# Keeping the results of seven batches in SBUF and storing them once, behind all loads

## The chip, the cores and the metric

The kernel runs on one core of one Trainium2 chip. The metric is the time of one execution on the device in microseconds (us), the median of several runs. The profile is of one execution; its span, from the first to the last instruction of the program, is some 1.8 us shorter than that time. The engines are PE (matmul), DVE (VectorE), ACT (ScalarE), POOL (GpSimd) and SP (SyncE, which here only issues DMAs and waits for them). SBUF is the memory on the chip that they work in; the tiles here take up to 128 of its partitions (rows). Transfers between SBUF and HBM, the large memory, are DMAs: the page counts 16 DMA engines, which carry them out in packets, here mostly of 1 to 16 KB (10,319 of the 11,744 packets on the page of the kernel before; the others are under 512 B).

## The reference

```python
B, S, D, H = 8, 2048, 2048, 8
x_heads = x.reshape(B, S, H, Dh).transpose(0, 2, 1, 3)     # Dh = 256
x_heads = x_heads + bias[None, :, None, :]
x_tiled = np.repeat(x_heads, 2, axis=2)                    # every result twice
mx = x_tiled.max(axis=-1, keepdims=True)
lse = mx.squeeze(-1) + np.log(np.exp(x_tiled - mx).sum(axis=-1))   # (8, 8, 4096), float32
```

For each of 8 x 2048 rows and 8 heads it is the log of a sum of 256 exponentials. The input is 134.2 MB, the output 1.05 MB (1.0 MB if a MB is 2^20 bytes): eight batches of 128 KB of results.

## The kernel before

One batch is eight tiles of 256 rows (2 MB each), so there are T = 64 tiles, in nine buffers. SP issues the loads in order. A part of each row gets its bias on PE and is summed by ACT; the rest goes through POOL, ACT's exp and DVE's sum. Two tiles after the end of batch b, `finish(b)` transposes that batch's sums, takes the Ln of them twice over and stores 64 rows of 2 KB. The store is issued on SP, so it stands in the same queue as the loads:

```python
res = [sb.tile([H * NBLK, P, K, 2], F32, name=f"res{i}") for i in range(2)]
...
def finish(b):
    ...
    nc.scalar.activation(out=rs[0:nr], in_=tv, func=ACT.Ln)
    nc.sync.dma_start(
        out=out[b].rearrange("h (n r) -> (h n) r", r=n),
        in_=rs[0:nr].rearrange("q p k r -> q (p k r)"),
    )
...
for t in range(T):
    ...                                    # compute on tile t, load tile t + NBUF
    fb, at = divmod(t - 2, NBLK)
    if fb >= 0 and at == NBLK - 1:
        finish(fb)
for_pe and for_pe()                        # the sums of the last row
finish_last()                              # batch 7: transpose, Ln, the last store
```

(Cuts are marked with "...".) The last batch takes another path (`finish_last`), with 128 rows of 1 KB; the change does not touch it. The last tiles are loaded in smaller pieces, and from tile 49 on the work is shared out differently, so that less is left to do when the last byte is in.

The softmax here doesn't subtract the row's maximum and nothing guards it: scores larger than these inputs give would overflow.

## Time and profile before

| | before |
|---|---|
| time, median of 3 | 332.10 us (332.07 to 332.19) |
| span of the profiled run | 330.5 us |
| stores among the loads / behind them | 6 / 2 |
| issue of the last store, and from there to the end | 327.13 us, 3.35 us |

The main views are in the prediction. One more, from the page's part on DMA issues: what was issued, how often, KB each, and the median us from issue to landing.

```profile
xt<-in_x_dram SPq DMA_DIRECT2D x57, 2048.0 KB, 31.8
...
out_dram<-res SPq DMA_DIRECT2D x7, 128.0 KB, 31.3
...
out_dram<-res_last SPq DMA_DIRECT2D x1, 128.0 KB, 1.7
```

A store of 128 KB needs 1.7 us where the queue is empty (last line) and 31.3 us among the loads (middle line). Nobody waits for it there (the trace lists no waiter for `out_dram`). What it costs is the time it takes from the loads behind it, and that this view does not show; it is in the spacing of the loads, 4.89 us from one 2 MB load to the next and about 5.19 across a store.

### The profile page before, as it was taken

The page shows a single profiled execution, that of the slowest core. Times are in us where ns is not written, and L with a number is a line of the kernel's source. Part 1 is how long each engine was busy: PE and PEld are TensorE (multiplying, and loading weights), DVE is VectorE, ACT ScalarE, POOL GpSimd, SP SyncE. Part 2 cuts the span into 40 slices and gives each one's busy share as a digit, 9 for nine tenths or more (in the row PEclk, how much of TensorE's full clock was granted, in tenths as well). Part 3 has the DMA queues.
Part 4 walks back from the last instruction along what each step waited for, and adds up shares of the span by engine and source line. Part 5 has one row for each costly group of instructions (what it writes and reads, how often), then busy time and mean ns, then how long its engine had stood idle before and what let it go on. Part 6 is the DMA issues. An engine that isn't in the chain of part 4 may idle for free.

```text
span 330.5 us, 2287 instructions
## 1 busy us (share of the span) xinstructions
PE 228.9 (69%) x383; PEld 65.3 (20%) x383; DVE 288.3 (87%) x380; ACT 291.4 (88%) x567; POOL 270.7 (82%) x79
## 2 busy tenths in 40 slices
PE   6498675695759667689667796866686645665780
PEld 2132121121212221222211221221121110132220
DVE  0019999999999999999999999998889999999994
ACT  3279999899999999989999889998999998999894
POOL 6999999979989999899999999988998667786300
PEclk9997977579775977955898558777857555555585
DMA  7999999999999999999999999999999999999970
GB/s 293 433 426 434 426 429 426 430 424 428 420 435 425 430 428 426 431 427 430 425 428 426 428 428 428 428 428 427 428 428 429 426 432 415 421 420 421 418 277 17
DMA packets 11744, 135.42 MB, mean 410 GB/s; under 512 B 1425, under 2 KB 1553, under 8 KB 2769
## 3 DMA queue, kind: packets, MB, share of 16 engines
q1 hardware_dynamic: 11632, 135.27, 96.9%
q14 instruction: 11, 0.09, 0.1%
q8 instruction: 3, 0.05, 0.1%
q10 hardware_dynamic: 2, 0.01, 0.0%
q0 software_dynamic: 96, 0.00, 0.0%
HBM read 134.23 MB, written 1.05 MB: 409 GB/s over the span
## 4 chain that ended last, share of the span: by engine, by line
DMA 61%; ACT 14%; issue 7%; POOL 6%; PE 6%; DVE 5%; DVEq 0%; POOLq 0%; SPq 0%; ACTq 0%
DMA xt<-in_x_dram 58%; ACT xt L212 10%; PE ps L177 4%; POOL xt L207 4%; ACT ps L189 4%; DVE xt L222 3%; DVE R L228 2%; DMA b<-bparts 2%; PE ps L167 1%; DMA brow<-in_bias_dram 1%; DVE junk L240 1%; POOL brest L132 0%; POOL brest L130 0%; POOL b L135 0%; PE tpair L258 0%
## 5 line engine op out<-in xcount | busy, mean ns | idle before, releaser
L207 POOL TENSOR_TENSOR xt<-xt,b_rep 128x2048 f32<-128x2048 f32 (+2 forms) x65 | 264.3, 4068 | 35.9 <-DMA xt<-in_x_dram 26.9
L177 PE MATMUL ps<-xt,ident 128*128 128x512 f32 (+1 forms) x240 | 174.6, 859 | 72.1 <-DMA xt<-in_x_dram 71.7
L212 ACT ACTIVATE xt<-xt 128x3072 f32<-128x3072 f32 (+3 forms) x89 | 184.6, 2095 | 10.0 <-POOL xt L207 8.1
L228 DVE TENSOR_REDUCE R<-xt 128x12 f32<-128x3072 f32 (+1 forms) x56 | 176.6, 3154 | 5.8 <-DVE xt L222 1.0
L189 ACT ACTIVATE ps<-ps 128x256 f32<-128x256 f32 x232 | 85.7, 369 | 15.5 <-PE ps L177 10.8
L222 DVE TENSOR_TENSOR xt<-xt,w_ps 128x1024 f32<-128x1024 f32 x49 | 59.6, 1217 | 29.9 <-ACT xt L212 29.8
L177 PEld LDWEIGHTS ps<-xt,ident 128*128 128x128 f32 x240 | 53.5, 252 | 153.9 <-DMA xt<-in_x_dram 113.6
L167 PE MATMUL ps<-b,ones 3*128 3x512 bf16 (+1 forms) x120 | 48.7, 471 | 9.9 <-ACT ps L189 6.0
L189 ACT ACTIVATION_READ_ACCUMULATOR ps<-ps 128x1 f32 x232 | 44.1, 190 | 0.0
L240 DVE CUSTOM_DVE_ANT_0 junk<-xt,w_ps 128x256 f32<-128x256 f32 x114 | 40.6, 417 | 1.2 <-ACT xt L212 1.1
L167 PEld LDWEIGHTS <-ones 3*128 3x128 bf16 x120 | 7.8, 98 | 79.7 <-issue 79.7
L228 DVE TENSOR_REDUCE R_last<-xt 128x3 f32<-128x768 f32 (+1 forms) x9 | 9.4, 1042 | 0.0
L258 PE MATMUL tpair<-ident,R 128*64 128x128 f32 x14 | 3.7, 360 | 7.7 <-DVE R L228 6.2
L240 DVE CUSTOM_DVE_ANT_0 junk<-xt,w_sb 128x256 f32<-128x256 f32 x18 | 6.7, 422 | 0.0
L240 DVE DVE_READ_ACCUMULATOR2_ANT R_last<- 128x1 f32 x76 | 6.5, 85 | 0.0
L139 PE MATMUL ps<-brow,ones 1*128 1x512 f32 x4 | 3.7, 1088 | 3.2 <-DMA brow<-in_bias_dram 3.2
L145 ACT ACTIVATE b_rep<-ps 128x512 f32<-128x512 f32 x2 | 1.2, 598 | 4.4 <-PE ps L139 4.4
L240 DVE DVE_READ_ACCUMULATOR2_ANT R<- 128x1 f32 x56 | 4.7, 84 | 0.0
L268 ACT ACTIVATE res<-tpair 64x512 f32<-64x512 f32 x7 | 4.1, 581 | 0.4 <-PE tpair L258 0.4
L139 PE MATMUL w_ps<-brow,ones 1*128 1x512 f32 x4 | 4.0, 1096 | 0.7 <-ACT w_ps L151 0.7
L258 PEld LDWEIGHTS tpair<-ident,R 128*64 128x64 f32 x14 | 1.4, 134 | 14.9 <-DVE R L228 11.9
L151 ACT ACTIVATE w_ps<-w_ps 128x512 f32<-128x512 f32 x2 | 1.2, 582 | 3.3 <-PE w_ps L139 3.3
(21 smaller groups left out, 12.4 us busy)
## 6 DMA issues: line engine op xcount, KB each, us to landing
xt<-in_x_dram SPq DMA_DIRECT2D x57, 2048.0 KB, 31.8
xt<-in_x_dram SPq DMA_DIRECT2D x12, 1024.0 KB, 20.8
out_dram<-res SPq DMA_DIRECT2D x7, 128.0 KB, 31.3
xt<-in_x_dram SPq DMA_DIRECT2D x3, 256.0 KB, 15.7
xt<-in_x_dram SPq DMA_DIRECT2D x2, 384.0 KB, 15.9
xt<-in_x_dram SPq DMA_DIRECT2D x1, 512.0 KB, 12.2
out_dram<-res_last SPq DMA_DIRECT2D x1, 128.0 KB, 1.7
b<-bparts POOLq DMA_DIRECT2D x3, 1.0 KB, 5.8
```

Of the source, the lines that this page charges most:

```text
L139: nc.tensor.matmul(dst, lhsT=ones, rhs=brow[:, c0:c1], start=True, stop=True)
L145: nc.scalar.activation(out=b_rep[:, c - G0 : c - G0 + MM], in_=ps[i], func=ACT.Copy)
L167: nc.tensor.matmul(p[:, 0 : (kb - ka) * n], lhsT=ones3, rhs=each_row(b3, 0, n, kb - ka), start=True, stop=False,)
L177: nc.tensor.matmul(bass.AP(tensor=p.tensor, offset=p.offset, ap=[p.ap[0], [1, (kb - ka) * n]]), lhsT=ident, rhs=xt[:, ka:kb, 0:n], start=F ...
L189: nc.scalar.activation(out=p[:, c : c + Dh], in_=p[:, c : c + Dh], func=ACT.Exp, accum_out=dst(h),)
L207: nc.gpsimd.tensor_tensor(out=v, in0=v, in1=each_row(b_rep, c - G0, D - c, k1 - k0), op=ALU.add)
L212: nc.scalar.activation(out=v, in_=v, func=ACT.Exp)
L222: nc.vector.tensor_tensor(out=f, in0=f, in1=each_row(w_ps, h0 * Dh - W0, n, k1 - k0), op=ALU.mult,)
L228: nc.vector.tensor_reduce(out=sums[:, k0:k1, h0:H], in_=v.rearrange("p k (h j) -> p k h j", j=Dh), op=ALU.add, axis=mybir.AxisListType.X,)
L240: nc.vector.tensor_tensor_reduce(out=j, in0=v, in1=w, scale=1.0, scalar=0.0, op0=ALU.mult, op1=ALU.add, accum_out=dst,)
L258: nc.tensor.transpose(out=tp[0:nr, k], in_=R[b][:, k].rearrange("p h n -> p (h n)"), identity=ident,)
L268: nc.scalar.activation(out=rs[0:nr], in_=tv, func=ACT.Ln)
```

## The change

Its intent: take the stores out of the load stream. Each Ln writes to its own part of a larger tile, and one store of 64 x 7 rows of 2 KB is issued after the seventh Ln, when SP has issued all loads.

```diff
-    res = [sb.tile([H * NBLK, P, K, 2], F32, name=f"res{i}") for i in range(2)]
+    res = sb.tile([H * NBLK, B - 1, P, K, 2], F32, name="res")
...
-        nc.scalar.activation(out=rs[0:nr], in_=tv, func=ACT.Ln)
+        nc.scalar.activation(out=res[:, b], in_=tv, func=ACT.Ln)
+
+    def store():
+
         nc.sync.dma_start(
-            out=out[b].rearrange("h (n r) -> (h n) r", r=n),
-            in_=rs[0:nr].rearrange("q p k r -> q (p k r)"),
+            out=out[0 : B - 1].rearrange("b h (n r) -> (h n) b r", n=NBLK),
+            in_=res.rearrange("q b p k r -> q b (p k r)"),
         )
...
             finish(fb)
+            if fb == B - 2:
+                store()
```

More of the change, by code (lines that the diff above doesn't have):

```diff
@@ L253, in finish @@
         nr = H * NBLK
-        n = P * K * 2
         tp = tps[b % 2]
-        rs = res[b % 2]
         for k in range(K):
```

## The prediction

> **What bounds the kernel now.** I began with the page's head, the rows by slice and the memory totals:
>
> ```profile
> span 330.5 us, 2287 instructions
> ...
> DMA  7999999999999999999999999999999999999970
> GB/s 293 433 426 434 426 429 426 430 424 428 420 435 425 430 428 426 431 427 430 425 428 426 428 428 428 428 428 427 428 428 429 426 432 415 421 420 421 418 277 17
> ...
> HBM read 134.23 MB, written 1.05 MB: 409 GB/s over the span
> ```
>
> The reader is to see that the 16 DMA engines are full in slices 2 to 38 (8.26 us each) and move some 427 GB/s whatever the compute stage: 135.28 MB / 427 GB/s = 317 us of 330.5 is transfer. The page's chain says the same, 61% of the span being DMA and 58% loads of x. Next, the stages:
>
> ```profile
> 137.00:176.00 39.00, 30.37 (x49) 8.76 (x50) 36.17 (x16) 36.13 (x72) 35.84 (x9) 0.70 1.01 428
> ...
> 255.00:290.00 35.00, 19.30 (x24) 4.70 (x23) 34.90 (x122) 31.83 (x48) 24.55 (x8) 0.50 1.00 424
> 290.00:300.00 10.00, 5.76 (x14) 2.30 (x13) 10.00 (x42) 9.82 (x18) 7.34 (x5) 0.50 1.01 421
> 300.00:310.00 10.00, 6.43 (x13) 2.45 (x13) 10.00 (x40) 9.28 (x17) 7.26 (x4) 0.50 1.02 423
> 310.00:318.00 8.00, 7.76 (x11) 1.98 (x11) 7.87 (x42) 6.86 (x13) 0.00 (x0) 0.60 1.01 405
> 318.00:326.10 8.10, 3.30 (x8) 0.78 (x6) 7.01 (x40) 7.20 (x21) 0.00 (x0) 0.82 0.22 84
> ```
>
> Columns: stretch, its length, busy us of PE, PE weight loads, DVE, ACT, POOL (instructions in brackets), granted TensorE clock, DMA share, GB/s. In the bulk (137 to 176) DVE, ACT and POOL have 2.8 to 3.2 us of slack in 39 while DMA has none. From 255 to 318 DVE has only 0.23 us of slack in 63: it works off a backlog, but the DMA share stays at 1.00 or more, so it does not hold the loads back. The last row is the tail: loads are ending, and DVE and ACT finish the last tile.
>
> Third, the chain of waits in order of time, near its end, and the issues of the DMA queue:
>
> ```profile
> 304.94 15.24 DMA xt<-in_x_dram
> ...
> 322.97 0.95 ACT xt L212
> ...
> 326.24 0.46 PE tpair L276
> 326.70 0.02 issue
> 326.72 0.38 ACT res_last L282
> ```
>
> ```profile
> 219.71 0.47 SPq L269 DMA_DIRECT2D out_dram<-res  x1
> 224.20 35.98 SPq L103 DMA_DIRECT2D xt<-in_x_dram  x9
> 262.06 0.47 SPq L269 DMA_DIRECT2D out_dram<-res  x1
> 266.95 45.72 SPq L103 DMA_DIRECT2D xt<-in_x_dram  x16
> 314.88 0.47 SPq L269 DMA_DIRECT2D out_dram<-res  x1
> 327.13 0.35 SPq L283 DMA_DIRECT2D out_dram<-res_last  x1
> ```
>
> A piece of the last tile lands at 320.18; 6.55 us of ACT and DVE follow, then transpose, Ln, and the last store's issue at 327.13. That store lands 1.7 us later (DMA issues part of the page). The second view holds the point of this case: the seventh store, at 314.88, already comes after the last load was issued (by 312.7). Only **six** of the seven stores lie among the loads.
>
> [...]DMA share 1.01, and a store's bytes take their time from the loads. [...]a 128 KB store lands 31.3 us after issue (median), about as long as the 31.8 us of a 2 MB load, so it queues behind the loads in flight. [...]the 2 KB store packets among the loads took 0.084 us, as did 2 KB load packets (the trace's DMA packet records), but a store alone on all engines does not occur before the change except at 1/7 of the size.
>
> **The change part by part.**
>
> *Removed from the load stream.* Six stores of 64 rows of 2 KB. By bytes: 6 x 0.131 MB = 0.786 MB, / 427 GB/s = 1.84 us. By packets: 64 x 0.084 us / 16 engines = 0.336 us a store, 2.0 us for six. By cadence, from the completion records of the loads: two 2 MB loads complete 4.89 us apart, with a store between them 5.19 to 5.20, so 0.30 to 0.31 us a store, 1.8 us for six. I choose **1.85 us**: the last load lands that much earlier.
>
> *Removed from the DMA queue's instructions.* Six issues of 0.47 us on SP. They are worth nothing: SP's issues of loads wait 224.1 us in total for DVE to free a tile (the DMA queue's own waits), and some six loads are in flight behind every issue (31.8 us to landing / 4.9 us a tile).
>
> *Moved.* The seventh store was behind all loads and stays there; nothing is saved for it.
>
> *Added.* One store of 64 x 7 rows of 2 KB, 0.918 MB, issued when the seventh Ln is long done and SP has issued its last load, near 313. It starts engine by engine as each ends its loads. By packet time: 448 x 0.084 / 16 = 2.35 us[...]. The packet records have most DMA engines free of loads at about 319 and one or two lagging until 321.6; take off 1.85: 317.2 and 319.8. [...] The last store is not issued before 327.13 - 1.85 = 325.3. It is therefore **hidden**[...]; its completion wait at the program's end runs beside that of the last store.
>
> *Unchanged.* Seven Ln of 0.58 us on ACT and 14 transposes on PE. The buffers of the results grow from 2 x 2 KB to 7 x 2 KB a partition; that shifts addresses, to which I give no time.
>
> *Does the tail follow the loads?* DVE is saturated from 255.9 to about 316, and the sixth store's data moves at 288 (packet records), so its 0.31 us reaches DVE only once DVE has caught up. It has: it idles 0.29, 0.37 and 0.42 us for ACT's exp at 318.8, 321.4 and 323.9. The first five stores precede the saturated stretch and shift it as a whole. ACT's exp, in turn, follows the piece landed at 320.18. So I carry the full 1.85 us to the end: 332.1 - 1.85 = 330.25, and round up for what may be lost: **330.3 us**, 0.5% less.
>
> **The rivals.**
>
> 1. *The merged store becomes the end of the chain.* For it: it is 7 times as large[...]. [...] If its rate were a quarter of the loads'[...], 0.918 / 107 = 8.6 us, it would end near 328, the last store behind it would land some 1.5 us later than before, and the kernel would take about 332 to 333.
>
> 2. *It disturbs the last loads.* Engines that are done early write the store to HBM while the lagging ones still load. For it: before the change the seventh store did the same for a seventh of the time. Against it: the packet times of load and store did not lengthen each other in the six earlier meetings. If the lag grew by half a microsecond, 330.8.
>
> 3. *Another engine takes the bound and swallows the gain.* For it: in the stretch 310 to 318 DVE and PE are nearly full; the granted clock is 0.50 until about 316.4, then 1.0, and if that moment stays fixed, work that comes 1.85 us earlier meets the slow clock: two matmuls of 128x512 take 2.07 us there and 1.12 after it. Against it: PE then still has 0.99 us (weight loads) of waiting for the last pieces to make it up. If it all counted, half the gain would go: 331.2. In the bulk this rival is weak: ACT's and DVE's 36.2 us in 39 leave 7%, and the change asks for 0.8% at most.
>
> 4. *The store was hidden anyway.* It would be if the DMA engines had gaps. A share of 1.01 and a cadence that stretches by 0.30 us at each store speak against it. It would leave 332.1.
>
> **Range and chances.** The gain's three estimates run from 1.8 to 2.0 us: 330.1 to 330.3. Runs of one kernel lie within 0.12 us of one another. What can go wrong goes upward mostly: rivals 2 and 3 cost 0.5 to 1. A lower end of 329.7 allows 0.4 us for smaller lag at the end. An upper end of 331.6 holds rivals 2 and 3 but not 1 or 4. Faster by over 2% would need 6.6 us, over three times the stores' whole transfer time: 1%. Slower by over 2% would need the merged store to end at about 333: 1%. Within 2%: 98%.
>
> **What would show each step.** In the profile of the changed kernel: 134.2 MB read and 1.05 MB written as before; one store issue of 896 KB, at about 313 and no issue of stores among the loads; the load cadence at 4.89 us without the five or six stretched steps; the last x piece on the chain landing at about 318.3; the last store's issue at about 325.3, landing in 1.7 us; span about 328.6. If the loads land 1.85 us earlier and the issue of the last store does not, rival 3 holds, and DVE or PE will show no idle time in the last 10 us. If the last store's time to landing grows well past 1.7 us, rival 1 holds. If the loads land less than 1.5 us earlier, the cost of a store among loads was mis-sized, or rival 2 or 4 holds: rival 2 would lengthen packets only after 313.

The sum: 332.1 - 1.85 = 330.25, rounded up to 330.3 us. By the packet time, 2.35 us, the store ends at 319.8 + 2.35 = 322.2, and 325.3 - 322.2 = 3.1 us are to spare.

That a store starts engine by engine, as each ends its loads, agrees with the landing records, 16 to each of these transfers (which engine each belongs to they do not say). In the kernel before, those of the last load lie at 318.79 to 322.72 us and those of the seventh store at 319.06 to 323.05, each 0.27 to 0.37 after the load's of the same rank. In the changed kernel they are 317.06 to 321.21 and 319.46 to 323.40, each 2.1 to 2.6 later. So the first parts of the store have landed while the last parts of the loads have not. They also put the end of the lagging engines, before the change, later than the 321.6 of the prediction: the last packets of 2 KB come in two rows, each of eight and then four, as a sixteenth of that load and of that store; the later row's eight end at 322.2.

## The result, and the profile after

The changed kernel took 330.00 us (median of 4 runs, 329.92 to 330.06), the kernel before in the same rounds 332.13 us (332.07 to 332.19). The ratio is 0.9936, 95% interval 0.9918 to 0.9953. (A ratio is the mean time of one kernel's fast runs over that of the other's of the same rounds, so not quite the ratio of the medians.) That is 2.13 us less; the prediction was 330.3 us.

The head of the changed kernel's page, as shown of the kernel before:

```profile
span 328.3 us, 2272 instructions
...
DMA  7999999999999999999999999999999999999991
GB/s 292 434 429 431 427 426 429 427 427 429 429 424 428 427 433 427 424 426 427 432 429 423 427 427 433 425 433 422 427 431 424 431 429 417 422 416 424 417 371 36
```

The DMA engines are as full as before, at the same 427 GB/s. Only the last slices differ: in the slice before the last 371 GB/s instead of 277, for the merged store now fills it (283 in the run below that leaves this store out). The rows by stage (columns as in the prediction):

```profile
255.00:290.00 35.00, 19.59 (x24) 4.79 (x24) 35.00 (x127) 31.86 (x49) 25.43 (x8) 0.50 1.01 425
...
310.00:318.00 8.00, 8.00 (x12) 1.96 (x11) 7.99 (x44) 6.94 (x15) 0.00 (x0) 0.54 1.02 401
318.00:326.10 8.10, 2.91 (x6) 0.79 (x6) 5.69 (x34) 6.00 (x19) 0.00 (x0) 0.88 0.26 95
```

DVE still has no slack from 255 to 318, and the DMA share is still 1.01 or more there. The stretch has moved: it begins 1.1 us sooner (at 254.76 instead of 255.87), and DVE's last two waits for ACT come 1.6 us sooner (at 319.76 and 322.33 instead of 321.37 and 323.94). Next, all issues of SP's DMA queue, and the landing of the merged store from the page:

```profile
0.74 310.25 SPq L103 DMA_DIRECT2D xt<-in_x_dram  x75
313.22 0.71 SPq L270 DMA_DIRECT2D out_dram<-res  x1
325.53 0.37 SPq L284 DMA_DIRECT2D out_dram<-res_last  x1
```

```profile
out_dram<-res SPq DMA_DIRECT2D x1, 896.0 KB, 10.2
```

The loads are now one unbroken run. The merged store is issued at 313.22 and lands 10.2 us later, at 323.4: 2.1 us before the last store is issued. And the chain of waits near the end, to be held against 304.94, 322.97, 326.24 and 326.72 in the prediction:

```profile
303.25 15.48 DMA xt<-in_x_dram
...
321.36 0.95 ACT xt L212
...
324.63 0.46 PE tpair L277
325.09 0.02 issue
325.12 0.39 ACT res_last L283
```

The piece that had landed at 320.18 lands at 318.73, and the last Ln starts at 325.12 instead of 326.72. So 1.60 us of the gain arise before the last store. The span fell by 2.19 us, though: **another 0.59 us lie behind the issue of the last store** (3.35 us before, 2.76 after), where the prediction had put nothing.

Where the loads win can be read from the packet records. The table counts, from the start, how many 2 MB loads' worth of x had landed, and when. (Packets of 8 KB and more, in order of their ends.)

| loads landed | before, us | changed, us | difference |
|---|---|---|---|
| 16 | 81.56 | 81.52 | 0.04 |
| 22 | 111.32 | 111.02 | 0.30 |
| 31 | 155.74 | 155.17 | 0.57 |
| 40 | 200.30 | 199.40 | 0.90 |
| 49 | 244.65 | 243.47 | 1.19 |
| 55 | 274.34 | 272.85 | 1.49 |
| 61 | 304.38 | 302.64 | 1.74 |

Six steps of 0.29 us in the mean, one for each removed store, and between them the difference changes by less than 0.1 us. Each step lies where the store's bytes come up, some 25 to 30 us after its issue.

### The profile page after: what moved, and what is told of

Same layout as the page of the kernel before. It is cut to its first block, busy times and chain, and to the rows that moved or that the text cites. A ratio compares the mean times of both kernels' runs of the same rounds, so it can differ in the third digit from the quotient of the medians.

```text
span 328.3 us, 2272 instructions
## 1 busy us (share of the span) xinstructions
PE 227.3 (69%) x383; PEld 65.9 (20%) x383; DVE 287.8 (88%) x380; ACT 290.9 (89%) x567; POOL 270.6 (82%) x79
## 5 line engine op out<-in xcount | busy, mean ns | idle before, releaser
L212 ACT ACTIVATE xt<-xt 128x3072 f32<-128x3072 f32 (+3 forms) x89 | 184.6, 2095 | 10.4 <-POOL xt L207 8.9
L189 ACT ACTIVATE ps<-ps 128x256 f32<-128x256 f32 x232 | 85.7, 370 | 14.0 <-PE ps L177 9.5
L189 ACT ACTIVATION_READ_ACCUMULATOR ps<-ps 128x1 f32 x232 | 44.1, 190 | 0.0
L240 DVE DVE_READ_ACCUMULATOR2_ANT R_last<- 128x1 f32 x76 | 5.8, 77 | 0.0
## 6 DMA issues: line engine op xcount, KB each, us to landing
out_dram<-res SPq DMA_DIRECT2D x1, 896.0 KB, 10.2
```

Of the source, the lines that this page charges most:

```text
L189: nc.scalar.activation(out=p[:, c : c + Dh], in_=p[:, c : c + Dh], func=ACT.Exp, accum_out=dst(h),)
L212: nc.scalar.activation(out=v, in_=v, func=ACT.Exp)
L240: nc.vector.tensor_tensor_reduce(out=j, in0=v, in1=w, scale=1.0, scalar=0.0, op0=ALU.mult, op1=ALU.add, accum_out=dst,)
```

## The experiments

Theory 1: a store costs what its bytes take in the full load stream, about 0.3 us, and what counts is only *where* it stands. Theory 2, a rival: each store has a fixed cost, and *merging* is what helps. Theory 3: the 0.59 us at the end come from the number of DMA instructions on the queue. Twelve kernels were run; the times of the kernel before beside them were 332.19 to 332.25 us.

**Moved, not merged.** Seven single stores, all behind the loads.

```diff
-                store()
+                for sb_ in range(B - 1):
+                    store(sb_, sb_ + 1)
```

> Seven single stores of 128 KB, all issued after the last load. Theory 1 (bytes among the loads: a store costs 0.30 us of the load stream where it stands there, however it is cut): the last store is issued as in the changed kernel, at 325.5, 1.6 us before that of the kernel before. Theory 2 (a fixed cost for each store, which only merging saves): the last store is issued at 327.1, as in the kernel before. Theory 3 (0.55 us of the gain arise after the last store's issue, from the number of DMA instructions on the queue, here 84 as in the kernel before): from that issue to the end 3.3 us again instead of 2.8. Theories 1 and 3 together: 330.5 us; theory 2: 332; theory 1 without 3: 330.0.

Measured: 329.96 to 330.38, median 330.0 us, ratio 0.9938 (0.9926 to 0.9950).

```profile
313.05 8.02 SPq L270 DMA_DIRECT2D out_dram<-res  x7
325.24 0.36 SPq L284 DMA_DIRECT2D out_dram<-res_last  x1
```

The seven issues are spread over 8.02 us instead of 0.71, beside everything else. The time equals the changed kernel's: merging is not needed. Theory 3 fails: with 83 DMAs on SP, as before (84 with one of ACT's, as the expectation counts), only 2.87 us pass from the last store's issue to the end, not 3.35.

**Merged, not moved.** One store of six results where the sixth stood, in the midst of the loads.

```diff
-            if fb == B - 2:
-                store()
+            if fb == B - 3:
+                store(0, B - 2)
+            if fb == B - 2:
+                store(B - 2, B - 1)
```

> Six results in one store of 768 KB in the middle of the loads, right after the sixth batch; the seventh alone at the end. Theory 1: 0.786 MB still lie among the loads, so the last store is issued at 327.0 or some tenths sooner and the time is 331.4 to 332.1. Theory 2: the six fixed costs are gone, so 330.0. Theory 3: 79 DMA instructions, so the end after the issue of the last store may be either 2.8 or 3.3 us.

Measured: 331.81 us (331.69 to 331.83), ratio 0.9988 (0.9976 to 1.0001).

```profile
260.48 0.72 SPq L270 DMA_DIRECT2D out_dram<-res  x1
...
327.19 0.36 SPq L284 DMA_DIRECT2D out_dram<-res_last  x1
```

The last store is issued at 327.19, as in the kernel before (327.13). By the packet records the loads were 1.54 us ahead after 52 loads and 0.05 us *behind* after 61: the store at 260 gave it all back when its bytes came up, some 30 us later. So merging inside the stream saves nothing there, and theory 2 falls. What is left, 0.4 us with a ratio whose interval reaches 1, fits the shorter end (2.69 us instead of 3.35).

**Three in the stream.** Batches 0 to 2 are stored as before, 3 to 6 in one store behind the loads.

```diff
-            if fb == B - 2:
-                store()
+            if fb < 3:
+                store(fb, fb + 1)
+            if fb == B - 2:
+                store(3, B - 1)
```

> Three single stores stay among the loads, the other four batches leave in one store behind the loads. Theory 1: three times 0.27 to 0.30 us, so the last store is issued 0.8 to 0.9 us later than in the changed kernel, at 326.3 to 326.4; time 330.8 to 331.4 by what the end takes. If the gain were a step (one particular store that hurts, such as the sixth in the stretch where DVE is saturated), 330.0.

Measured: 331.05 us (330.60 to 331.24), ratio 0.9965 (0.9952 to 0.9977). The last store is issued at 326.59, 1.06 us later than in the changed kernel, somewhat more than expected; after 61 loads the stream is 0.92 us ahead of the kernel before, about half of 1.74. The cost goes by the store, and no single one of them holds it.

**No early results stored.** The call of the merged store is taken out; the result is wrong.

```diff
-            if fb == B - 2:
-                store()
```

> Wrong result on purpose: the results of the first seven batches are computed and never stored. If the merged store is hidden, as predicted, the last store is issued at 325.5 as in the changed kernel, and the time is 330.0 within 0.3. If the merged store disturbs the lagging loads or the end (rivals 1 and 2 of the prediction), the time falls below 329.5.

Measured: 329.92 us (329.75 to 330.09), ratio 0.9932 (0.9919 to 0.9946).

```profile
325.34 0.35 SPq L284 DMA_DIRECT2D out_dram<-res_last  x1
```

Leaving out 0.918 MB of stores altogether brings 0.1 us against the changed kernel, less than the 0.27 us by which two measurements of the same program differ (next run). The merged store is hidden within that scatter: neither rival 1 nor the 0.5 us of rival 2 shows.

**The store placed in the program after the last Ln.** An attempt to lay the store bare, which missed.

```diff
         nc.scalar.activation(out=res_last, in_=tv, func=ACT.Ln)
+        store()
         nc.sync.dma_start(                          # the last store
```

> The merged store is issued only after the last Ln, just ahead of the last store: its cost by itself, with no load beside it. At the packet time of 0.084 us, 448 packets on 16 engines take 2.35 us, so about 2.4 us plus 0.7 of issue more than the changed kernel: 332.5 to 333.1. [...] If it were much slower (rival 1 of the prediction), over 336.

Measured: 329.73 us (329.69 to 329.90), ratio 0.9927 (0.9913 to 0.9940). The profile shows the merged store issued at 312.93, as in the changed kernel (313.22), and the last store at 325.18: nothing held SP back until the last Ln. In the changed kernel the seventh Ln, whose result the store takes, had started at 293.56, and SP's last wait before the issue ended with the landing of a load, at 313.16. What ran was the changed kernel again. That is of use as a measure of scatter between jobs: the profiled last store issue was 325.18, not 325.53, and the median differs by 0.27 us.

**The store behind the last store.** The same, mended: now SP comes to it only after the last store, which waits for the last Ln.

```diff
     finish_last()
+    store()
```

> The merged store is issued after the last store, so that it really starts only when all else is done (in the earlier attempt SP issued it at 312.9, since nothing held it back). Packets at 0.084 us on 16 engines: 2.35 us more than a store of 128 KB needs, and 0.4 us of issue: 332.5 to 333. [...] Over 336: much slower alone than among loads.

Measured: 334.94 us (334.64 to 335.08), ratio 1.0079 (1.0066 to 1.0093).

```profile
325.59 0.35 SPq L284 DMA_DIRECT2D out_dram<-res_last  x1
325.99 0.71 SPq L270 DMA_DIRECT2D out_dram<-res  x1
```

```profile
out_dram<-res SPq DMA_DIRECT2D x1, 896.0 KB, 6.3
```

The time lies between the two branches of the expectation. The same bytes at the wrong place cost 4.9 us. The merged store's packets took 0.150 us each in the mean, where the same 2 KB packets among loads took 0.084: 448 x 0.150 / 16 = 4.2 us, or 0.918 MB / 4.2 us = 218 GB/s. That is about half of the loads' 427 GB/s. That writing to HBM halves the rate is unlikely: the last store, 128 rows of 1 KB on all 128 partitions, is by itself too, and its packets took 0.047 us, 128 x 1 KB / (8 x 0.047 us) = some 345 GB/s. The two stores differ in rows and in partitions, and no run stored 2 KB rows from 128 partitions, so the cause is not shown. In the changed kernel the median of all 2 KB packets from 316 on is still 0.084 us (mean 0.088); there part of it runs beside the last loads, and after 320 the DMA share is 0.3 or less, that is at most some 5 of 16 engines at a time.

**The seventh store in three.** The kernel before, with two more DMAs behind the loads, to test theory 3.

```diff
-        nc.sync.dma_start(out=out[b]..., in_=rs[0:nr]...)
+        cuts = [0, nr] if b < B - 2 else [0, 32, 48, nr]
+        for q0, q1 in zip(cuts, cuts[1:]):
+            nc.sync.dma_start(out=out[b]...[q0:q1], in_=rs[q0:q1]...)
```

> The kernel before, with its seventh store, which is behind the loads anyway, cut into three by rows, so that the queue carries 86 DMA instructions and the last store counts on the same semaphore as in the changed kernel. Theory 3 in the form that the semaphore decides: from the last store's issue to the end some 0.13 us less than before, 332.0 us. In the form that the number of instructions decides the 0.37 us that SP spends between two drains: either 3.2 or 2.8 us, the time 332.0 or 331.6. If neither: 332.1. The last store's issue stays at 327.1 in all of them.

Measured: 332.06 us (331.99 to 332.21), ratio 0.9997 (0.9984 to 1.0009); last store issued at 327.09, then 3.13 us. This is between the forms expected, but the trace told more. SP has a wait of 0.36 us which no recorded semaphore explains, and it stands at another place of the closing sequence than in the kernel before, though in both right after **SP's 207th recorded instruction**. The kernel before has 211 of them, the changed kernel 199; it never gets there. That became theory 4.

**Seven buffers alone.** The kernel before with seven result tiles and the stores where they were.

```diff
-    res = [sb.tile(...) for i in range(2)]
+    res = [sb.tile(...) for i in range(B - 1)]
...
-        rs = res[b % 2]
+        rs = res[b]
```

> The kernel before with seven result buffers instead of two, its stores where they were: the other part of the change alone. Theory 4 (SP stalls 0.36 us at its 207th recorded instruction, wherever the program stands then; the buffers' reuse costs SP six instructions, so that the kernel before reaches the 207th, with 211, and the changed kernel, with 199, does not): SP has 205, no stall, from the last store's issue to the end 2.9 us instead of 3.35, the last store's issue still at 327.1, 331.7 us. Without theory 4: 332.1.

Measured: 332.13 us (331.93 to 332.49), ratio 0.9997 (0.9984 to 1.0010). My expectation was wrong in one point: the instructions do not come from the buffers' reuse, since SP has 211 as before. The wait is there too, 0.34 us after the 207th, and 3.33 us pass from last issue to end. So this agrees with theory 4, and the larger buffers and shifted addresses cost or save nothing that the run could show (0.13%).

**Thirteen pieces.** The changed kernel, with its store in 13 pieces behind the loads; SP has 211 instructions again.

```diff
-                store()
+                for sb_ in range(B - 1):
+                    store(sb_, sb_ + 1, [0, 64] if sb_ == 0 else [0, 32, 64])
```

> The changed kernel with its store cut into 13 behind the loads, so that SP has 211 recorded instructions as the kernel before. Theory 4: a wait of about 0.36 us in front of the 208th, and 3.1 to 3.3 us from the last store's issue to the end instead of 2.76; 330.4 us. If the stall belongs to stores among the loads: 2.8 us and 330.0. Theory 1 in both: the last store's issue at 325.2 to 325.5, unless the 13 issues themselves run past it.

Measured: 330.53 us (330.38 to 330.70), ratio 0.9948 (0.9936 to 0.9961).

```profile
325.54 0.35 SPq L285 DMA_DIRECT2D out_dram<-res_last  x1
```

The last store is issued as in the changed kernel (325.53), yet 3.38 us pass to the end, a little more than expected. SP's drains at the end (durations in ns are least, median, most; then us of first and last start), in the kernel before, the changed kernel, and this one:

```profile
L373 SPq DRAIN  x3: 7/7/116, 329.2 to 330.0; - x3
```

```profile
L376 SPq DRAIN  x3: 7/7/7, 327.5 to 327.8; - x3
```

```profile
L378 SPq DRAIN  x3: 7/7/120, 327.7 to 328.4; - x3
```

The first and last drain lie 0.7 or 0.8 us apart with 211 instructions, and 0.3 with 199. The changed kernel has been given the old tail back, without one store among its loads. The wait follows the position in SP's program. In every kernel that passes the 207th it is there (0.34 to 0.37 us, six of six profiles); the other eight end before it, with 205 at most.

**A second transfer beside each store.** To double the dose of theory 1, the kernel before also loads 64 rows of 2 KB from x into a scratch tile after each of the six stores.

```diff
+        if b < B - 2:
+            nc.sync.dma_start(out=extra, in_=x[b, 0:nr, 0:MM])
```

> The kernel before, and beside each of the six stores among the loads a further transfer of the same 64 rows of 2 KB, from x into a scratch tile. Theory 1: twice the bytes, so the last store is issued 1.6 to 1.9 us later, at 328.7 to 329.0, time 333.7 to 334.2. If bytes among the loads cost nothing: 332.1.

Measured: 338.81 us (338.23 to 339.48), ratio 1.0200 (1.0186 to 1.0214). That is 6.6 us more, more than three times what was expected. The packets account for 5.3 us of it: those of the extra rows took 2.1 us (their time over 16 engines); the 16 KB packets of x, 7168 in each kernel, took 0.6226 us in the mean instead of 0.6164, which is 2.8 us over 16 engines; and the 8 KB packets took 0.4 us more. The other 1.3 us stay open. The longer packets stand around the extra loads: in the stretches of 10 us in which the first five of these moved, the mean was 0.64 to 0.67 us, elsewhere 0.615. The suspect, which nothing had shown so far, was the 64 partitions.

**The same dose on 128 partitions.** As before, with 128 rows of 1 KB.

```diff
+            nc.sync.dma_start(out=extra, in_=x[b, 0:P, 0:Dh])
```

> The second transfer beside each of the six stores again, now of 128 rows of 1 KB instead of 64 of 2 KB, the same bytes. In the run with 64 rows, 2.1 us of the 6.5 us were the extra packets' own time and 2.8 us were packets of x that took longer after them (16 KB packets 0.622 us in the mean, not 0.615). If the 64 partitions caused that, here only the bytes count: 1.8 to 2.4 us more than the kernel before, 334.0 to 334.6. If any small load among the large ones does it: 338 again.

Measured: 334.30 us (334.16 to 334.36), ratio 1.0062 (1.0048 to 1.0076), that is 2.1 us more, and the 16 KB packets are back at 0.6163 us. Six times 128 KB among the loads cost 2 us, coming in or going out: theory 1 at twice the dose. So the large loss belongs to *loads* of 64 rows of 2 KB. Whether the 64 partitions or the 2 KB do it, these two runs do not separate, for both changed. The 64-row stores of the kernel before had no such effect, its 16 KB packets taking 0.6164 us with them and 0.6168 in the changed kernel.

**The last sums at the end.** A version to beat both. In the changed kernel ACT works without a gap as the last pieces land, and two sums of the last tile's first row (line L189, 320.37 to 321.35) stand ahead of the last exp's (L212):

```profile
318.90 1.56 ACT L212 ACTIVATE xt<-xt 128x768 f32<-128x768 f32 x2
...
320.88 0.37 ACT L189 ACTIVATE ps<-ps 128x256 f32<-128x256 f32 x1
...
321.26 1.56 ACT L212 ACTIVATE xt<-xt 128x1024 f32<-128x1024 f32 x2
```

```diff
-                else:
+                elif t < T - 1:
                     for_pe = pe_part
+                else:
+                    at_end.append(pe_part)
...
-    for_pe and for_pe()
+    for part in at_end:
+        part()
```

> A version to beat both: the changed kernel, where ACT is busy without a gap from 315.7 to 320.4 and the last exp's stand behind two sums of the last tile's first row that nobody waits for yet; here these sums come after the last exp's. The last exp starts up to 1.0 us sooner; DVE had 1.1 us of idle time before its last groups; ACT then ends with four sums, 2.05 us, so the last transpose starts 0.5 to 0.9 us sooner: 329.1 to 329.5. If the landing of the last pieces sets the start of the last exp's: no gain.

Measured: 329.44 us (329.40 to 329.64), ratio 0.9917 (0.9904 to 0.9931), result correct. This is 0.56 us below the changed kernel's median, though in another job: against the kernel before of the same rounds the changed kernel had 0.9936, and the intervals of the two ratios overlap. The repeat of the changed kernel (329.73 us, 0.9927) halves the difference. So it is 0.3 to 0.6 us; the ranges of the runs do not meet.

```profile
318.68 1.56 ACT L212 ACTIVATE xt<-xt 128x768 f32<-128x768 f32 x2
320.53 1.57 ACT L212 ACTIVATE xt<-xt 128x1024 f32<-128x1024 f32 x2 [0.29 <-DMA xt<-in_x_dram]
322.01 0.36 ACT L189 ACTIVATE ps<-ps 128x256 f32<-128x256 f32 x1
```

The last exp's follow the first ones and now even wait 0.29 us for their load. They start 0.73 us sooner than above, 0.22 us of which the first exp's already had, and the last store's issue came at 324.87 (325.18 to 325.59 in the kernels with the unchanged last tile and no store among the loads).

## Why the prediction was right

**The bound** was read rightly. The load stream decides, at a share of 1.01 before and after; DVE's saturated stretch moved with it, and the steps of the table lie at the stores, including the sixth.

**Six of seven** was right. The kernel without any early store (325.34) and the changed kernel (325.53) issue the last store at the same time within scatter: a store behind the loads cost nothing here, even one of seven batches, so the seventh had nothing to give. The load stream, too, shows six steps and no more.

**The term of 1.85 us** came out at 1.74 us in the load stream after 61 loads, six steps of 0.29. It was 1.45 us at the landing of the chain's last piece (318.73, predicted about 318.3) and 1.60 us at the last store's issue (325.53, predicted 325.3). Six profiled kernels have no store among their loads and the unchanged last tile (the changed one, moved, none stored, the repeat, the store behind the last, thirteen pieces). Against 327.13 they issue the last store 1.54 to 1.95 us sooner, 1.73 in the mean. That 327.13 is one profile; the two kernels with the old load stream (seventh in three, seven buffers) have 327.09 and 326.86, and against the mean of the three it is 1.62. So the term was 0.1 to 0.2 us too large, and of its three estimates that by packets (2.0 us) was the farthest off; cadence and bytes (1.8) were better.

**The hidden store** was right. It landed at 323.4, 1.2 us after the 322.2 that the packet time gave and 1.9 us before the 325.3 at which the last store was predicted. By itself it ran at 218 GB/s (4.2 us), which no view before the change could show.

**Merging** was given nothing for fewer issues and fixed costs. That was right too: seven single stores behind the loads do as well.

**What was not in the sum** is the program's end, 0.59 us. Of it, 0.31 us is the wait after SP's 207th recorded instruction (0.36 us before; at the same place of the closing sequence 0.05 us pass after), shown by putting it back. The drain behind it took 116 ns instead of 7, 0.11 us. The last 0.17 us are SP's closing checks of semaphores: four came after that of the last store before the change, two after it. The reading of instruction counts, "worth nothing", held for the issues beside the loads, but not for the position of the closing sequence. The two misses were of opposite sign and partly cancelled: 1.60 + 0.59 = 2.19 us of span, where 1.85 was predicted. That the time came so near is in part luck: with the old end, the thirteen pieces took 330.53 us.

**Slips in the working.** The 6.55 us of "ACT and DVE" after the landing at 320.18 hold the transpose as well, for they end at 326.73; by the chain shown the transpose starts at 326.24, after 6.06 us. Rival 1's 332 to 333 us doesn't follow from a landing 1.5 us later than before, which would be 332.1 + 1.5 = 333.6. Neither was used in the sum.

**The rivals** found no support. The third (another engine swallows the gain) may have taken up to 0.14 us between the loads' 1.74 and the 1.60 at the end in that one profile; the scatter of 0.4 us among equal kernels doesn't let one say so. The clock did what this rival feared: it rose at 317.3 us (before: 316.4), and of PE's last twelve matmuls of 512 columns seven took 1.06 us or more, not five. Yet the last of them began 1.53 us sooner (319.87 instead of 321.40), so PE had room to make most of it up.

What the wait at the 207th instruction is stays open. The packet records hold a hint: in the six profiles with the wait, an 8 KB packet of the kind "instruction" starts 1.0 to 1.3 us after the end of the 207th, and in none of the other eight does one start between the last store's issue and the end of the span. But it starts when the wait (0.34 to 0.37 us) is already over, and the record doesn't say for which engine, so the cause is not shown.

## What to carry to other kernels

In this kernel, bound by its loads, a small store cost its transfer time in the stream (0.29 us for 128 KB), whether single or merged (six in one gave back the whole lead of 1.54 us). Queued behind the last load, where compute still runs and the DMA engines run empty, it was free (330.00 us with the merged store, 329.92 without any); queued behind the last result, it cost more than it ever did among the loads (4.9 us, against 1.7 for six of the seven among the loads). Look at what the program does after its last transfer as well: it is short, but nothing hides it (3.35 us from the last store's issue to the end before, 2.76 after: 0.59 of the 2.19 us won).
